# Order of the seven-product pairs, of the weight products and of the weight sums in a one-core decoder layer in float32

## The chip, the cores and the metric

One core of one Trainium2 chip runs the whole program. The metric is the device time of one execution in microseconds; a profiled execution has its own time, and a span from its first to its last instruction. PE is TensorE (its weight loads are listed as PEld), DVE is VectorE, ACT is ScalarE, POOL is GpSimd, SP is SyncE, which here only issues loads.

## The reference

One layer on 256 tokens of width 2048, all in float32:

```
h = rmsnorm(x);  z = h @ W_in            (forgetting attention, mLSTM and two gates)
merged = sigmoid(g_a) * (A @ P_A) + sigmoid(g_m) * (M @ P_M)
x = x + merged @ W_out
u = causal_dwconv3(rmsnorm(x) @ W_up)    (2 x 5632 columns)
x = x + (silu(u_gate) * u_val) @ W_down  (5632 x 2048)
```

The weights are read once; nearly all work is the matrix products.

## The kernel before, in words

**Two halves of each operand.** [...] A weight piece of 128 x 1024 comes from a 1 MB load (`raw`, two pieces each, three buffers, issued by SP); ACT makes the high part `wh` (line 169) and DVE the low part `wl` (line 170, raw minus high). Both have three buffers of 1024 columns. A product of two operands takes three TensorE products: low by high, high by high and high by low.

**Who looks ahead.** `next_sub` hands out the next weight piece and prepares those ahead: two pieces in all in the plain stages, three in the paired ones (`next_sub(3)` in `piece`, line 291). A scheduler then orders each engine's queue by priority and by its own view of when operands and buffers are there; the queues run in that order.

**The stages in order.** First `mog` (mLSTM output gate), then `fq`, `fk`, `fv`, `mq`, `mk`, `mv`, the gates `g0` to `g3`, the projections `p`, `wo0` and `wo1` (W_out), `up` (W_up, 88 blocks of 128 columns), `y0` and `y1` (W_down, 1024 columns each).

- In `mq`, `mk` and `up` (`products_a`, line 258) the weights are the stationary operand: for each of 16 slices of the inner dimension there is one product of 512 columns (high and low activations side by side, against `wh`) and one of 256 columns (high activations against `wl`). They alternate.
- In `g`, `wo` and `y` (`s_block`, line 277) the activations are stationary and the weights move, always 512 columns. The inner dimension goes in pairs of 256 rows. A pattern string says how each pair is multiplied: `p` is plain, eight block products or 24 TensorE products, in two weight pieces; `S` is a scheme with seven block products, 21 TensorE products in four weight pieces. `S` needs differences of weight blocks, which DVE makes in one tile `sums` (lines 154, 161 and 164), and sums of activation blocks.
- For `y` the activation sums are made in `up` by `put_sums`, written to DRAM by POOL, and read back two pairs at a time into tiles `s_ops`, by `load_sums` (line 947), also from POOL.

The pattern of `y` is `ppp` `SSpSp` `SSpSp` `SSpSp` `Sp` `pp`: 22 pairs, ten of them `S`. The patterns of `g1` to `g3` (`pSpSpSpp`) and `wo` (`pSpSpppp`) are not touched.

**The pool `a8`.** Tiles of 8 KB per partition share 15 buffers: among them the four tiles `h2` (normalised activations, read by every block of `up`), the eleven tiles `ghl` (output of `up`, filled one by one), `sums` and the tiles `s_ops`.

**Ends of the `y` stages.** The four sums of seven-product results are combined after the last `S` pair (`late`, two operations for each further weight piece), then the four quarters `q` are added (line 974) and written out by SP.

Of the kernel before, what the change touches and what calls it, by code (L numbers as in the profile page):

```python
# [1 line left out]

# [1 line left out]

# [31 lines left out]
PLAIN = "p" * 8  # L36
G_PAIRS = "pSpSpSpp"
WO_PAIRS = "pSpSpppp"
Y_PAIRS = "ppp" + "SSpSp" * 3 + "Sp" + "pp"
N_S = Y_PAIRS.count("S")  # L40


# [18 lines left out]
def trunk(ctx: ExitStack, tc: tile.TileContext, a):  # L61
# [14 lines left out]
        return psaux.tile([P, 512], F32, tag="aux", name=name)  # L76

    def a8(name, shape, dtype=F32):
        return big.tile([P, *shape], dtype, tag="a8", bufs=15, name=name)

    def scratch(name, shape, tag="w2k", bufs=4):
        return work.tile(shape, F32, tag=tag, bufs=bufs, name=name)
# [51 lines left out]
    def split_sub(j):  # L134
        if j >= len(subs_of) or j in subs:
            return
        i, s, kind = subs_of[j]
        load_chunk(i)
        if j < KD:
            put(hT[j][:, 0, :], hT[j][:, 1, :], xT[j], cst[:, C_G1 + j : C_G1 + j + 1])  # L140
        n = 512 if kind == "b21" else chunks[i][1] // 2
        raw, sums = raws[i], s_tiles.get("sums")


        if kind == "whole":
            src = raw[:, s * n : (s + 1) * n]
        elif kind == "b":
            src = raw[:, 512:1536]
            if s_tiles["of"] != chunks[i][2]:
                s_tiles["of"] = chunks[i][2]  # L150
                s_tiles["sums"] = a8(f"sums{i}", [2048])
            sums = s_tiles["sums"]
            with tc.issue_after(last_of["up"].ins) if "up" in last_of else nullcontext():
                nc.vector.tensor_tensor(  # L154
                    sums[:, :1024].rearrange("p (i c) -> p i c", i=2),
                    raw[:, :512].unsqueeze(1).to_broadcast([P, 2, 512]),
                    src.rearrange("p (i c) -> p i c", i=2), ALU.subtract,
                )
        elif kind == "b21":
            src = raw[:, 1536:]  # L160
            nc.vector.tensor_tensor(sums[:, 1024:1536], raw[:, 1024:1536], sums[:, :512], ALU.subtract)
        elif kind == "t13":
            src = sums[:, :1024]
            nc.vector.tensor_tensor(sums[:, 1536:], raw[:, 1536:], sums[:, 1024:1536], ALU.subtract)
        else:
            src = sums[:, 1024:]
        wh = wpool.tile([P, 1024], F32R, tag="wh", bufs=3, name=f"wh{j}")
        wl = wpool.tile([P, 1024], F32R, tag="wl", bufs=3, name=f"wl{j}")
        nc.scalar.activation(wh[:, :n], src, AF.Copy)  # L169
        nc.vector.tensor_tensor(wl[:, :n], src, wh[:, :n].bitcast(F32), ALU.subtract)  # L170
        subs[j] = (wh[:, :n], wl[:, :n])

    state = {"sub": 0}
# [83 lines left out]

    def products_a(z, act, ks, wh, wl, first, last):

        for q, k in enumerate(ks):  # L260
            ws = slice(q * P, (q + 1) * P)
            mm(z, wh[:, ws], act[k].rearrange("p l s -> p (l s)"), first and q == 0, False)
            mm(z[:, :S], wl[:, ws], act[k][:, 0, :], False, last and q == len(ks) - 1)

    def half_a(z, act, s, tasks_per_sub=1):
        wh, wl = next_sub()
# [10 lines left out]
    def s_block(name, pairs, s_ops, pattern, pools, dst, add=True, per_piece=0):  # L277


        q = [[pools[0](f"{name}q{tok}{h}") for h in range(2)] for tok in range(2)]  # L280
        ps, late, left = {}, [], pattern.count("S")
        n_s = left

        def prod(out, x, w, c, first, last):
            wh, wl = w[0][:, c * 512 : (c + 1) * 512], w[1][:, c * 512 : (c + 1) * 512]
            mm(out, x[1], wh, first, False)
            mm(out, x[0], wh, False, False)
            mm(out, x[0], wl, False, last)

        def piece():  # L290
            w = next_sub(3)
            for _ in range(min(2, len(late))):
                late.pop(0)()
            run_tasks(per_piece)
            return w

        def tt(o, x, y):
            late.append(lambda: nc.vector.tensor_tensor(o, x, y, ALU.add))

        for m, kind in enumerate(pattern):  # L300
            def op(i, tok):
                t = slice(tok * P, (tok + 1) * P)
                return pairs[m][:, i, 0, t], pairs[m][:, i, 1, t]

            if kind == "p":
                last = m == len(pattern) - 1
                ws = [piece(), piece()] if last else []

                todo = (
                    [(i, tok, h) for h in range(2) for tok in range(2) for i in range(2)] if last  # L310
                    else [(i, tok, h) for i in range(2) for h in range(2) for tok in range(2)]
                )
                for i, tok, h in todo:
                    if i == len(ws):
                        ws.append(piece())
                    prod(q[tok][h], op(i, tok), ws[i], 1 - h, m == 0 and i == 0, last and i == 1)
                continue
            first, last = left == n_s, left == 1
            left -= 1
            s1, s2, s3, s4 = s_ops[m]  # L320
            w = piece()
            if first:
                ps = {i: pools[1](f"{name}p{i}") for i in (1, 5, 7, 6)}
            prod(ps[1], op(0, 0), w, 0, first, last)
            prod(q[0][1], s4, w, 1, False, False)
            prod(q[0][0], op(1, 0), piece(), 0, False, False)
            w = piece()
            prod(ps[5], s1, w, 0, first, last)
            prod(ps[7], s3, w, 1, first, last)
            w = piece()  # L330
            prod(ps[6], s2, w, 0, first, last)
            prod(q[1][0], op(1, 1), w, 1, False, False)
            if not last:
                continue
            c11, c12, c21, c22 = (dst(tok, h) for tok in range(2) for h in range(2))
            u2 = scratch("u2", [P, 512])
            if add:
                u3 = scratch("u3", [P, 512])
                late.append(lambda: nc.scalar.activation(u2, ps[1], AF.Copy))
                tt(c11, c11, ps[1])  # L340
                tt(u2, u2, ps[6])
                tt(u3, u2, ps[7])
                tt(u2, u2, ps[5])
                tt(c21, c21, u3)
                tt(u3, u3, ps[5])
                tt(c12, c12, u2)
                tt(c22, c22, u3)
            else:
                late.append(lambda: nc.scalar.activation(c11, ps[1], AF.Copy))
                tt(u2, c11, ps[6])  # L350
                tt(c21, u2, ps[7])
                tt(c12, u2, ps[5])
                tt(c22, c21, ps[5])
        for f in late:
            f()
        return q
# [564 lines left out]
    for j in range(NF):  # L921
# [12 lines left out]
        if Y_PAIRS[m] == "S":  # L934
# [3 lines left out]
                s_dram[:, n_s * 6 * P : (n_s + 1) * 6 * P], se.rearrange("p l c -> p (l c)")  # L938
            )
            n_s += 1  # L940
        last_of["up"] = put_pair(g_pairs[m], gv)


    s_pos = [m for m, kind in enumerate(Y_PAIRS) if kind == "S"]
# [13 lines left out]
        at = [ring[r][:, q * P : (q + 1) * P] for q in range(6 * i, 6 * i + 6)]  # L958
        return [(g[:, 0, 0, P:], g[:, 0, 1, P:])] + [(at[c], at[3 + c]) for c in range(3)]

    for _ in range(2):
        load_sums()
    for b in range(2):
        pools = (acc_tile, aux_tile) if b == 0 else (aux_tile, acc_tile)
        xr = big.tile([P, 2, 1024], F32, tag="mv", name=f"xr{b}")
# [86 lines left out]
```

## Time and profile before

| | us |
|---|---|
| median of 3 runs | 1402.15 |
| lowest and highest run | 1394.18, 1404.11 |
| the profiled execution, its time | 1393.67 |
| the profiled execution, its span | 1391.9 |
| PE busy | 1375.6 |
| DVE busy | 1070.9 |
| ACT busy | 767.2 |

The granted TensorE clock is 1.000 over the span. A matmul's end is modelled in this profile: one of 512 columns is shown as 390 ns or so, though the next one starts sooner. What a stage costs is therefore read here from start to start, and a wait from a start that comes later than the rest, not from the busy shares.

### The profile page before, as it was taken

What the parts mean: (1) busy time and instruction counts of PE and PEld (TensorE: products, weight loads), DVE (VectorE), ACT (ScalarE), POOL (GpSimd) and SP (SyncE); (2) the same over time, 40 slices, a digit from 0 to 9 for tenths busy, and PEclk for the clock granted to TensorE, in tenths of its full rate; (3) what the DMA queues carried; (4) which work ended last, traced back from release to release, by engine and by line L of the source; (5) the groups of instructions that cost most, each with busy time, mean ns of one, the idle gap of its engine ahead of it and who ended that gap; (6) DMA issues with size and microseconds to landing.
All of it is one profiled execution on the core that took longest, in us unless ns stands there. A gap on an engine that the chain in (4) does not pass through costs nothing.

```text
span 1391.9 us, 18433 instructions
## 1 busy us (share of the span) xinstructions
PE 1375.6 (99%) x6940; PEld 1157.2 (83%) x6940; DVE 1070.9 (77%) x1524; ACT 767.2 (55%) x1096; POOL 40.4 (3%) x73
## 2 busy tenths in 40 slices
PE   9999999999999999999999999999999999999998
PEld 8878888887888888888888888888888887778776
DVE  5655766556888867777878888888878888887987
ACT  6645554444665544555655555555655655553553
POOL 2101000000000000000000000000000000000000
PEclk9999999999999999999999999999999999999999
DMA  8645454443554565555555655655555657668553
GB/s 312 229 165 184 179 209 155 152 151 134 196 215 182 214 241 194 190 220 203 191 186 194 218 193 190 222 186 196 201 212 194 230 196 266 226 251 291 205 209 119
DMA packets 44073, 281.76 MB, mean 202 GB/s; under 512 B 5008, under 2 KB 5024, under 8 KB 13264
## 3 DMA queue, kind: packets, MB, share of 16 engines
q1 hardware_dynamic: 39168, 260.20, 52.4%
q0 software_dynamic: 4672, 20.38, 4.2%
q8 instruction: 54, 0.88, 0.2%
q14 instruction: 35, 0.29, 0.1%
q10 hardware_dynamic: 144, 0.02, 0.0%
HBM read 272.45 MB, written 8.13 MB: 202 GB/s over the span
## 4 chain that ended last, share of the span: by engine, by line
PE 96%; DVE 1%; issue 1%; ACT 1%; DMA 1%; POOL 0%; DVEq 0%; ACTq 0%; POOLq 0%
PE up L230 35%; PE p L230 6%; PE y1q L230 6%; PE y0q L230 5%; PE mog L230 3%; PE fq L230 3%; PE mv L230 3%; PE fk L230 3%; PE fv L230 3%; PE wo0q L230 3%; PE wo1q L230 3%; PE g1q L230 2%; PE g3q L230 2%; PE g2q L230 2%; PE g0q L230 2%; PE y1p L230 2%
## 5 line engine op out<-in xcount | busy, mean ns | idle before, releaser
L169 ACT ACTIVATE wh<-raw 128x1024 fp32r<-128x1024 f32 (+2 forms) x496 | 502.7, 1017 | 473.9 <-PE up L230 117.9
L170 DVE TENSOR_TENSOR wl<-raw,wh 128x1024 fp32r<-128x1024 f32 (+2 forms) x496 | 575.1, 1169 | 205.3 <-ACT wh L169 203.5
L230 PE MATMUL up<-h,wh 128*128 128x512 f32 x1408 | 488.6, 394 | 0.0
L230 PE MATMUL up<-h,wl 128*128 128x256 f32 x1408 | 390.0, 277 | 0.0
L230 PEld LDWEIGHTS up<-h,wh 128*128 128x128 f32 x1408 | 263.9, 188 | 61.4 <-DVE h L199 0.2
L230 PEld LDWEIGHTS up<-h,wl 128*128 128x128 f32 x1408 | 264.4, 188 | 0.1
L170 DVE TENSOR_TENSOR wl<-sums,wh 128x1024 fp32r<-128x1024 f32 x66 | 80.6, 1222 | 43.9 <-ACT wh L169 43.5
L169 ACT ACTIVATE wh<-sums 128x1024 fp32r<-128x1024 f32 x66 | 69.9, 1060 | 78.6 <-PE y0q L230 16.6
L909 DVE SCALAR_TENSOR_TENSOR t<-u,cst,t 128x256 f32<-128x256 f32 x176 | 84.7, 481 | 3.8 <-ACT t L907 0.7
L230 PE MATMUL p<-wh,am 128*128 128x512 f32 x256 | 79.6, 392 | 0.0
L230 PE MATMUL y1q<-wh,ghl 128*128 128x512 f32 x232 | 71.7, 390 | 0.0
L230 PE MATMUL y0q<-wh,ghl 128*128 128x512 f32 x232 | 71.7, 390 | 0.0
L230 PEld LDWEIGHTS p<-wh,am 128*128 128x128 f32 x256 | 47.6, 188 | 9.7
L907 ACT ACTIVATE t<-u,cst 128x256 f32<-128x256 f32 x88 | 52.0, 591 | 2.4 <-DVE u L904 1.9
L230 PEld LDWEIGHTS y1q<-wh,ghl 128*128 128x128 f32 x232 | 43.6, 188 | 9.2
L230 PEld LDWEIGHTS y0q<-wh,ghl 128*128 128x128 f32 x232 | 43.5, 188 | 9.1
L230 PE MATMUL p<-wl,am 128*128 128x512 f32 x128 | 49.9, 390 | 0.0
L230 PE MATMUL y1q<-wl,ghl 128*128 128x512 f32 x116 | 44.8, 391 | 0.0
L230 PE MATMUL y0q<-wl,ghl 128*128 128x512 f32 x116 | 44.8, 390 | 0.0
L154 DVE TENSOR_TENSOR sums<-raw 128x1024 f32<-128x1024 f32 x33 | 40.4, 1223 | 4.7 <-DMA raw<-in_w_dn 3.0
L230 PE MATMUL mog<-wh,hT 128*128 128x348 f32 (+1 forms) x192 | 42.4, 331 | 1.3 <-ACT wh L169 1.3
L230 PE MATMUL g0q<-wh,hN 128*128 128x512 f32 x128 | 41.3, 401 | 0.0
(370 smaller groups left out, 2064.0 us busy)
## 6 DMA issues: line engine op xcount, KB each, us to landing
raw<-in_w_up SPq DMA_DIRECT2D x88, 1024.0 KB, 4.9
raw<-in_w_dn SPq DMA_DIRECT2D x44, 1024.0 KB, 4.9
raw<-in_w_g SPq DMA_DIRECT2D x32, 1024.0 KB, 4.9
raw<-in_w_fox SPq DMA_DIRECT2D x24, 1024.0 KB, 4.9
raw<-in_w_p SPq DMA_DIRECT2D x16, 1024.0 KB, 4.8
raw<-in_w_out SPq DMA_DIRECT2D x16, 1024.0 KB, 4.8
raw<-in_w_mqk SPq DMA_DIRECT2D x8, 1024.0 KB, 4.8
raw<-in_w_mv SPq DMA_DIRECT2D x8, 1024.0 KB, 4.8
```

The source lines that it names most:

```text
L154: nc.vector.tensor_tensor(sums[:, :1024].rearrange("p (i c) -> p i c", i=2), raw[:, :512].unsqueeze(1).to_broadcast([P, 2, 512]), src.rear ...
L169: nc.scalar.activation(wh[:, :n], src, AF.Copy)
L170: nc.vector.tensor_tensor(wl[:, :n], src, wh[:, :n].bitcast(F32), ALU.subtract)
L230: nc.tensor.matmul(out, lhsT, rhs, start=start, stop=stop)
L907: nc.scalar.activation(t, u[:, 2:], AF.Identity, scale=w[2], bias=w[3])
L909: nc.vector.scalar_tensor_tensor(out=t, in0=u[:, i : i + S], scalar=w[i], in1=t, op0=ALU.mult, op1=ALU.add)
```

## The change

Five edits:

1. `Y_PAIRS` becomes `p`, ten times `Sp`, `p`: still 22 pairs and ten `S`, now at every second place.
2. `wh` and `wl` have four buffers in place of three, and `s_block` prepares four pieces ahead.
3. The pool `a8` has 14 buffers in place of 15, and one `s_ops` tile is loaded ahead in place of two.
4. The first operation of a seven-product pair's sums is queued behind the last low part issued so far (`issue_after`), in every paired stage; before, it was held only behind the last activation pair of `up`.
5. `products_a` takes two slices at a time: two products of 512 columns, then their two of 256.

```diff
-Y_PAIRS = "ppp" + "SSpSp" * 3 + "Sp" + "pp"
+Y_PAIRS = "p" + "Sp" * 10 + "p"
...
-        return big.tile([P, *shape], dtype, tag="a8", bufs=15, name=name)
+        return big.tile([P, *shape], dtype, tag="a8", bufs=14, name=name)
...
-            with tc.issue_after(last_of["up"].ins) if "up" in last_of else nullcontext():
+
+            with tc.issue_after(last_of["wl"].ins):
...
-        wh = wpool.tile([P, 1024], F32R, tag="wh", bufs=3, name=f"wh{j}")
-        wl = wpool.tile([P, 1024], F32R, tag="wl", bufs=3, name=f"wl{j}")
+        wh = wpool.tile([P, 1024], F32R, tag="wh", bufs=4, name=f"wh{j}")
+        wl = wpool.tile([P, 1024], F32R, tag="wl", bufs=4, name=f"wl{j}")
         nc.scalar.activation(wh[:, :n], src, AF.Copy)
-        nc.vector.tensor_tensor(wl[:, :n], src, wh[:, :n].bitcast(F32), ALU.subtract)
+        last_of["wl"] = nc.vector.tensor_tensor(
+            wl[:, :n], src, wh[:, :n].bitcast(F32), ALU.subtract
+        )
...
-        for q, k in enumerate(ks):
-            ws = slice(q * P, (q + 1) * P)
-            mm(z, wh[:, ws], act[k].rearrange("p l s -> p (l s)"), first and q == 0, False)
-            mm(z[:, :S], wl[:, ws], act[k][:, 0, :], False, last and q == len(ks) - 1)
+
+        for q in range(0, len(ks), 2):
+            two = [(slice(i * P, (i + 1) * P), act[ks[i]]) for i in (q, q + 1)]
+            for i, (ws, x) in enumerate(two):
+                mm(z, wh[:, ws], x.rearrange("p l s -> p (l s)"), first and q + i == 0, False)
+            for i, (ws, x) in enumerate(two):
+                mm(z[:, :S], wl[:, ws], x[:, 0, :], False, last and q + i == len(ks) - 1)
...
-            w = next_sub(3)
+            w = next_sub(4)
...
-        last_of["up"] = put_pair(g_pairs[m], gv)
+        put_pair(g_pairs[m], gv)
...
-    for _ in range(2):
-        load_sums()
+    load_sums()
```

Three places show how the queues move. The first is PE inside a block of `up`. Before:

```order
L230 MATMUL up_5923<-h_4789,wh_5893 128x512
L230 MATMUL up_5923<-h_4789,wl_5894 128x256
L230 MATMUL up_5923<-h_4789,wh_5893 128x512
L230 MATMUL up_5923<-h_4789,wl_5894 128x256
L230 MATMUL up_5923<-h_4789,wh_5893 128x512
```

and now (x2: two rows that read alike):

```order
L233 MATMUL up_6199<-h_4789,wh_6168 128x512 x2
L233 MATMUL up_6199<-h_4789,wl_6169 128x256 x2
L233 MATMUL up_6199<-h_4789,wh_6168 128x512 x2
L233 MATMUL up_6199<-h_4789,wl_6169 128x256 x2
L233 MATMUL up_6199<-h_4790,wh_6202 128x512 x2
```

The products are the same and as many; only their order in a group of four differs, and each still has a weight load of its own.

The second is DVE in `y0`. The number behind `raw` is the load, that behind `wl` the piece; four pieces belong to an `S` pair and two to a `p` pair. Before, at the second of two adjacent `S` pairs (`raw208`):

```order
L170 TENSOR_TENSOR wl442_10452<-sums207_10411,wh442_10451 128x1024
L154 TENSOR_TENSOR sums207_10411<-raw208_10409 128x1024
L170 TENSOR_TENSOR wl443_10466<-sums207_10411,wh443_10465 128x1024
L170 TENSOR_TENSOR wl444_10474<-raw208_10409,wh444_10473 128x1024
L161 TENSOR_TENSOR sums207_10411<-raw208_10409,sums207_10411 128x512
L170 TENSOR_TENSOR wl445_10485<-raw208_10409,wh445_10484 128x512
L164 TENSOR_TENSOR sums207_10411<-raw208_10409,sums207_10411 128x512
L170 TENSOR_TENSOR wl446_10498<-sums207_10411,wh446_10497 128x1024
L170 TENSOR_TENSOR wl447_10508<-sums207_10411,wh447_10507 128x1024
```

and now, from a `p` pair (`raw206`) through an `S` pair (`raw207`) to the next `p` pair (`raw208`):

```order
L171 TENSOR_TENSOR wl440_10400<-raw206_10335,wh440_10399 128x1024
L171 TENSOR_TENSOR wl441_10407<-raw206_10335,wh441_10406 128x1024
L155 TENSOR_TENSOR sums205_10341<-raw207_10383 128x1024
L171 TENSOR_TENSOR wl442_10418<-raw207_10383,wh442_10417 128x1024
L162 TENSOR_TENSOR sums205_10341<-raw207_10383,sums205_10341 128x512
L171 TENSOR_TENSOR wl443_10431<-raw207_10383,wh443_10430 128x512
L165 TENSOR_TENSOR sums205_10341<-raw207_10383,sums205_10341 128x512
L171 TENSOR_TENSOR wl444_10448<-sums205_10341,wh444_10447 128x1024
L171 TENSOR_TENSOR wl445_10466<-sums205_10341,wh445_10465 128x1024
L171 TENSOR_TENSOR wl446_10476<-raw208_10427,wh446_10475 128x1024
L171 TENSOR_TENSOR wl447_10483<-raw208_10427,wh447_10482 128x1024
```

The eight operations of an `S` pair are the same; what stands between two such groups is now always the two low parts of a `p` pair.

The third is ACT at the end of `up` (blocks up84 to up87 are its last; `wh434` is the first piece of `y0`). Before:

```order
L169 ACTIVATE wh430_10190<-raw202_10115 128x1024
L195 ACTIVATE ghl10_5500<-gv_10005 128x2x256
L360 ACTIVATE sum_10157<-up84_10114 128x256
L169 ACTIVATE wh431_10223<-raw202_10115 128x1024
L907 ACTIVATE t_10161<-u0_5502,cst_75 128x256
L169 ACTIVATE wh432_10243<-raw203_10168 128x1024
```

and now:

```order
L170 ACTIVATE wh435_10337<-raw204_10221 128x1024
L366 ACTIVATE sum_10263<-up86_10220 128x256
L198 ACTIVATE ghl10_5504<-gv_10005 128x2x256
L170 ACTIVATE wh436_10343<-raw205_10274 128x1024
L913 ACTIVATE t_10267<-u2_5508,cst_75 128x256
L170 ACTIVATE wh437_10348<-raw205_10274 128x512
L933 ACTIVATE sg_10271<-t_10267 128x256
L366 ACTIVATE sum_10316<-up87_10273 128x256
L170 ACTIVATE wh438_10365<-sums205_10341 128x1024
```

With 14 buffers the eleventh `ghl` tile takes the place of the first `h2` tile that block up87 has finished with, so its first half is written two blocks later than before; `sums` and the first `s_ops` tile take the next `h2` tiles in the same way. Behind it on ACT's queue stand the pieces of the first `S` pair of `y0` (`wh436` to `wh439`).

More of the change, by code (lines that the diff above doesn't have):

```diff
@@ L1 @@
-from contextlib import ExitStack, nullcontext
+from contextlib import ExitStack
 import numpy as np
```

## Prediction

> **What bounds the kernel now.** I read the page first: engines, then the chain that ended last.
>
> ```profile
> span 1391.9 us, 18433 instructions
> PE 1375.6 (99%) x6940; PEld 1157.2 (83%) x6940; DVE 1070.9 (77%) x1524; ACT 767.2 (55%) x1096; POOL 40.4 (3%) x73
> PE 96%; DVE 1%; issue 1%; ACT 1%; DMA 1%; POOL 0%; DVEq 0%; ACTq 0%; POOLq 0%
> ```
>
> TensorE holds the chain for 96% of the span. No edit removes a product, so only two things can be won: stretches in which PE stands still, and time lost between products. To see the stretches I need the step of an undisturbed stream. The timeline of PE, in the projections:
>
> ```profile
> 499.67 0.39 PE L230 MATMUL p<-wh,am 128*128 128x512 f32 x1
> ...
> 500.58 0.39 PE L230 MATMUL p<-wl,am 128*128 128x512 f32 x1
> ```
>
> Four products lie between these starts (the rows left out hold the second, third and fourth): 0.91/4 = 0.227 us a step for 512 columns. Then the view by tile, which gives first and last starts of a stage's products:
>
> ```profile
> L230 PE MATMUL g1q<-wh,hN x92: 387/389/400, 356.1 to 397.4; 128*128 128x512 f32 x92
> L230 PE MATMUL g2q<-wh,hN x92: 387/389/397, 397.9 to 439.5; 128*128 128x512 f32 x92
> L230 PE MATMUL y0q<-wh,ghl x232: 387/389/399, 1150.7 to 1269.3; 128*128 128x512 f32 x116
> L230 PE MATMUL y1q<-wh,ghl x232: 387/389/398, 1269.8 to 1386.7; 128*128 128x512 f32 x116
> ```
>
> A `y` stage has 12 plain pairs of 24 products and 10 `S` pairs of 21: 498 products, 113.0 us at 0.227. `y0` takes 1269.8 - 1150.7 = 119.1 us, so **6.1 us** are lost. `y1`, from its first start to 1386.7, where its last but one product starts, takes 116.9 us for 496 steps (112.6): **4.3 us** lost. Together 10.4. The stage `g1`, with three `S` pairs that each stand alone, has 183 products (41.5 us) and takes 397.9 - 356.1 = 41.8 us: 0.3 us lost, a tenth of a microsecond for each `S`.
>
> Where `y0` loses is in the timelines. PE, ACT and DVE at the second of two adjacent `S` pairs:
>
> ```profile
> 1174.48 0.63 PE L230 MATMUL y0p<-wh,s_ops 128*128 128x512 f32 x2
> 1175.92 0.51 PE L230 MATMUL y0p<-wh,s_ops 128*128 128x512 f32 x1 [0.81 <-ACT wh L169]
> ```
>
> ```profile
> 1174.81 1.06 ACT L169 ACTIVATE wh<-sums 128x1024 fp32r<-128x1024 f32 x1 [1.90 <-DVE sums L164]
> ```
>
> ```profile
> 1169.39 1.23 DVE L154 TENSOR_TENSOR sums<-raw 128x1024 f32<-128x1024 f32 x1
> 1170.54 1.22 DVE L170 TENSOR_TENSOR wl<-sums,wh 128x1024 fp32r<-128x1024 f32 x1
> 1171.67 1.22 DVE L170 TENSOR_TENSOR wl<-raw,wh 128x1024 fp32r<-128x1024 f32 x1
> 1172.81 0.68 DVE L161 TENSOR_TENSOR sums<-raw,sums 128x512 f32<-128x512 f32 x1
> 1173.41 0.68 DVE L170 TENSOR_TENSOR wl<-raw,wh 128x512 fp32r<-128x512 f32 x1
> 1174.01 0.68 DVE L164 TENSOR_TENSOR sums<-raw,sums 128x512 f32<-128x512 f32 x1
> 1174.61 2.51 DVE L170 TENSOR_TENSOR wl<-sums,wh 128x1024 fp32r<-128x1024 f32 x2
> 1177.04 1.22 DVE L170 TENSOR_TENSOR wl<-raw,wh 128x1024 fp32r<-128x1024 f32 x1
> ```
>
> Three starts of PE fit from 1174.48 to 1175.92, 1.44 us for two steps of 0.227: about 1 us stands still. It waits for a high part on ACT, which waits for the last sum on DVE, and DVE is the one that is late: from start to start its `S` group takes 1.15 + 1.14 + 0.60 + 0.60 + 0.60 + 2.43 = 6.5 us, against 21 x 0.227 = 4.8 us of PE. Two in a row put DVE 3.4 us behind. A `p` pair gives DVE 2 x 1.14 = 2.3 us of work in 24 x 0.227 = 5.4 us, which makes that good. The waits of both `y` stages, grouped:
>
> ```profile
> ACT wh L169 <- DVE sums L164: 11.4, 6, 1.9
> PEld y0p L230 <- DVE wl L170: 3.7, 10, 1.9
> PEld y0p L230 <- ACT wh L169: 3.7, 3, 1.2
> PEld y1p L230 <- ACT wh L169: 3.7, 3, 1.2
> PEld y1p L230 <- DVE wl L170: 2.1, 10, 0.3
> ```
>
> Six such waits for the six adjacent pairs, three per stage. The rows that count ten are a small wait at every `S`; the 1.9 us one in `y0` comes, in the chain of waits, behind a weight load that DVE released late:
>
> ```profile
> 1232.65 7.81 DMA raw<-in_w_dn
> ```
>
> **The change part by part.** The sum is against the profiled execution, 1393.67 us: the span of 1391.9 and 1.8 around it. That execution lies at the bottom of the runs shown (1394.18 to 1404.11, median 1402.15); I carry the difference over to the median.
>
> *One `S` at every second place.* Per `Sp` DVE works 6.5 + 2.3 = 8.8 us and PE 4.8 + 5.4 = 10.2 us, so DVE gains 1.4 us with each, and no `S` starts behind another. The six stops go, and the load of 1232.65, whose buffer was freed late by the same backlog, comes in time. What should be left is what `g1` shows, 0.1 us for each of 20 `S`: 2 us; with four buffers it may fall to nothing, because a high part then no longer waits for the piece just before. Of 10.4 us lost, 8.4 come back.
>
> *The start of `y0`.* The first `S` is now at the second place. The covers are used up here: at the end of `up`, DVE and ACT still finish two blocks, and the `sums` and `s_ops` tiles come only from `h2` tiles that block up87 leaves. ACT's queue stands for the first `ghl` half until the first `h2` tile is free, a quarter into that block, some 1 us; behind it are `wh436` to `wh439`, needed from 1150.7 + 5.4 = 1156.1 on, so this is hidden. The `s_ops` tile is needed at the second product group, 1156.1 + 0.7 = 1156.8. Before, the first went out here:
>
> ```profile
> 1147.02 0.57 POOL L952 DMA_DIRECT2D s_ops<-s_dram  x1 [43.80 <-PE up L230]
> ```
>
> ```profile
> DMA to landing us min/median/max: 4.4/4.7/10.6
> ```
>
> Now it waits for the third `h2` tile (the first goes to `ghl`, the second to `sums`), three quarters into up87, which takes 5.5 us to 1150.7: 1149.3, and 0.6 to issue. With the median it lands at 1154.6 and costs nothing; with the maximum at 1160.5 it costs 3.7. A weight load and the second `s_ops` run beside it, which puts it between: I take **0.7 us lost**, and 0 to 3.7 as ends.
>
> *From `y0` to `y1`.* Behind the last `S` come two `p` pairs and the first of `y1`, then again an `S`. The additions of line 974 wait for the last products, and the first sums of `y1` are queued behind them; but they are needed two pieces into a stage, 5.4 us later. I cost it at nothing; if that cover were gone, two additions and two sums, 4 x 0.6 = 2.4 us.
>
> *One `s_ops` ahead, 14 buffers elsewhere.* A tile serves two `S`, 20.4 us, and takes 4.7 to land: hidden. Before `up` the queues shift by single rows; 0, and 1 either way.
>
> *Sums behind low parts, four ahead, in `g` and `wo`.* `g1` loses 0.3 us as above, and `g2` 0.5 (397.9 to 439.5 is 41.6 us, for 181 steps that make 41.1), so little is to be had: 0.3 us gained, 0 to 1.
>
> *Products in groups of four.* There are 88 x 16 = 1408 pairs in `up` and 128 in `mq` and `mk`: 768 groups. The alternation, and a place where the scheduler happens to have put two and two:
>
> ```profile
> 799.89 0.39 PE L230 MATMUL up<-h,wh 128*128 128x512 f32 x1
> 800.12 0.27 PE L230 MATMUL up<-h,wl 128*128 128x256 f32 x1
> ...
> 801.62 0.40 PE L230 MATMUL up<-h,wh 128*128 128x512 f32 x1
> ```
>
> ```profile
> 665.50 0.40 PE L230 MATMUL up<-h,wh 128*128 128x512 f32 x1
> 665.86 0.62 PE L230 MATMUL up<-h,wh 128*128 128x512 f32 x2
> 666.32 0.40 PE L230 MATMUL up<-h,wl 128*128 128x256 f32 x2
> 666.55 0.40 PE L230 MATMUL up<-h,wh 128*128 128x512 f32 x1
> ```
>
> Five pairs from 799.89 to 801.62 are 0.346 us each, 0.692 for two. A 512 step is 0.23 there against 0.227 in `p`; half of 0.227 and the whole make 0.3405, so 5.5 ns a pair are lost to something. If a neighbour of the other length costs them, groups of four save half: 5.5 ns x 768 = 4.2 us. If every product has the same fixed cost, they save nothing. The group of four in the trace takes 666.55 - 665.86 = 0.69 us: no gain against two settled pairs, 0.03 against its neighbour pair (665.86 - 665.50 = 0.36). So the ends are 0 and 4.2, nearer 0: **1.3 us gained**.
>
> [...]
>
> Sum: -8.4 + 0.7 - 0.3 - 1.3 = **-9.3 us**: 1384.4 beside the profiled 1393.67, and 1402.15 - 9.3 = **1392.9** beside the median.
>
> **The rivals.**
>
> *The order of the products is worth nothing.* Every product has its fixed cost; the one group of four speaks for it, the longer 0.23 against it. Time 1392.9 + 1.3 = 1394.2.
>
> *The order is worth more.* All that `up`, `mq` and `mk` lose between unlike products goes: 5.5 ns x 1536 = 8.4 us in place of 1.3, so 1385.8. The group of four speaks against it.
>
> *`y` keeps half its losses.* The tile `sums` is still single, and DVE is busy for most of the stage:
>
> ```profile
> 1150.70:1269.80 119.10, 115.24 (x501) 91.82 (x500) 101.80 (x112) 63.56 (x69) 3.19 (x6) 1.00 0.68 246
> ```
>
> 101.8 of 119.1 us. If the late `s_ops` tile costs its 3.7 and each `S` still loses 0.2 us (4 of the 10.4), the sum is -6.4 + 3.7 - 0.3 - 1.3 = -4.3: 1397.9. Against it stands `g1`, with the same `Sp` and less buffering.
>
> *Slower: two short products in a row uncover a weight load.* The costliest groups show how long a load lasts:
>
> ```profile
> L230 PEld LDWEIGHTS up<-h,wl 128*128 128x128 f32 x1408 | 264.4, 188 | 0.1
> ```
>
> 188 ns, and a 256 step is 0.115. Were the second load of two not hidden, each group would pay 188 - 115 = 73 ns, 768 x 73 = 56 us: 1449 us. It decides from (9.3 - 1.3)/768 = 10 ns a group on, where the gain is gone. The two short products from 666.32 to 666.55, 0.115 each, speak against it; and in the alternation too each short product covers one whole load.
>
> *Nothing changes.* The stops of `y` move elsewhere, as into the load queue: 1402.
>
> **How the numbers follow.** Chances: the forecast 0.42, the order worth nothing 0.24, the order worth more 0.10, half the losses 0.15, slower 0.04, nothing 0.05. The likeliest time is 1392.9. The runs of before spread over 10 us, so the range takes the cases from 1385.8 to 1397.9 and some 3 to 4 us of that spread on each side: 1382 to 1401. A change of 1%, 14 us, is about what a measurement of this kernel tells from none. Faster than that (under 1388.1) are the third case and what the spread makes of the first two, 0.20; slower by 1% only the fifth, 0.05; within 1%, 0.75.
>
> **What would show it.** In the profile after: `y0` and `y1` at 114 to 115 us each, no wait of ACT for DVE's third sum that PE feels, and no PE start more than 0.4 us late at an `S`. `up` from first to last start at 487 to 489 us if order is worth little, 480 if it is worth all, over 500 if loads are uncovered. The first `s_ops` landing before 1157. Wrong would be: `y` still over 117 us, or a new stop of several microseconds between `up` and the first `S`.

## The result, and the profile after

The changed kernel takes **1380.98 us** (median of 6 runs, 1380.65 to 1381.26); the kernel before, beside it, 1404.01 (6 runs, 1394.18 to 1405.35). The ratio is 0.985, 95% interval 0.982 to 0.987: faster by 1.5%. The forecast was 1392.9, and its range ended at 1382, one microsecond above the result.

The page of the changed kernel (span, engines, chain that ended last):

```profile
span 1379.4 us, 18385 instructions
PE 1369.1 (99%) x6940; PEld 1161.6 (84%) x6940; DVE 1069.6 (78%) x1524; ACT 766.7 (56%) x1096; POOL 40.9 (3%) x73
PE 96%; issue 1%; DMA 1%; DVE 1%; POOL 1%; ACT 0%; SPq 0%; DVEq 0%; ACTq 0%; POOLq 0%
```

The shares are as before; what has changed is when products start. The view by tile, with the first and last starts of a stage's products:

```profile
L233 PE MATMUL g1q<-wh,hN x92: 389/389/389, 354.5 to 395.5; 128*128 128x512 f32 x92
L233 PE MATMUL g2q<-wh,hN x92: 389/389/389, 396.0 to 437.0; 128*128 128x512 f32 x92
L233 PE MATMUL up<-h,wh x1408: 388/396/582, 657.9 to 1148.5; 128*128 128x512 f32 x176
L233 PE MATMUL up<-h,wl x1408: 274/277/287, 658.5 to 1148.9; 128*128 128x256 f32 x176
L233 PE MATMUL y0q<-wh,ghl x232: 389/389/395, 1149.0 to 1261.4; 128*128 128x512 f32 x116
L233 PE MATMUL y1q<-wh,ghl x232: 389/389/389, 1261.9 to 1374.3; 128*128 128x512 f32 x116
L233 PE MATMUL y1q<-wl,ghl x116: 388/389/389, 1262.3 to 1374.5; 128*128 128x512 f32 x116
```

`y0` takes 1261.9 - 1149.0 = 112.9 us (119.1 before); both `y` stages, from the first start of `y0` to the last of `y1`, 1374.5 - 1149.0 = 225.5 (before 1386.9 - 1150.7 = 236.2, its last start being that of the row below). That is 995 steps of 0.227: nothing is lost. `g1` takes 41.5 (41.8 before), also without loss. But `up` takes 1148.9 - 657.9 = 491.0, where before it took 488.7:

```profile
L230 PE MATMUL up<-h,wl x1408: 274/280/284, 662.2 to 1150.6; 128*128 128x256 f32 x176
L230 PE MATMUL y1q<-wl,ghl x116: 387/389/445, 1270.2 to 1386.9; 128*128 128x512 f32 x116
```

From the profiled execution of before to that of after, the span falls by 12.5 us. The medians differ by 23.0. Ten microseconds are thus not to be seen between these two profiles, and the experiments had to find them too.

DVE's timeline in `y0`, at one `S` pair:

```profile
1175.95 1.23 DVE L171 TENSOR_TENSOR wl<-sums,wh 128x1024 fp32r<-128x1024 f32 x1 [1.26 <-ACT wh L170]
1177.32 2.36 DVE L171 TENSOR_TENSOR wl<-raw,wh 128x1024 fp32r<-128x1024 f32 x2
1179.59 1.22 DVE L155 TENSOR_TENSOR sums<-raw 128x1024 f32<-128x1024 f32 x1
1180.73 1.22 DVE L171 TENSOR_TENSOR wl<-raw,wh 128x1024 fp32r<-128x1024 f32 x1
...
1183.67 1.22 DVE L171 TENSOR_TENSOR wl<-sums,wh 128x1024 fp32r<-128x1024 f32 x1
1186.15 1.23 DVE L171 TENSOR_TENSOR wl<-sums,wh 128x1024 fp32r<-128x1024 f32 x1 [1.26 <-ACT wh L170]
```

DVE now finishes the `S` pair, does the two low parts of the `p` pair and then begins the next sums, with 1.3 us to spare in each round (its wait for ACT). An `S` pair gives it seven operations, three sums and four low parts, not eight as the text ahead of the prediction has it; the 6.5 us of the prediction are those of the seven. The load of the first `s_ops` tile was feared to be late. POOL issues it at 1146.66, it lands 7.1 us later, at 1153.7, and PE first uses it at 1155.12:

```profile
1146.66 0.56 POOL L958 DMA_DIRECT2D s_ops<-s_dram  x1 [26.45 <-PE up L233]
```

```profile
1154.89 0.39 PE L233 MATMUL y0p<-wl,ghl 128*128 128x512 f32 x1
1155.12 0.62 PE L233 MATMUL y0q<-wh,s_ops 128*128 128x512 f32 x2
```

That product follows the one before it at the usual step of 0.23 us.

### The profile page after: what moved, and what is told of

Read it like the earlier page. It is cut to its first block, busy times and chain, and to the rows that moved or that the text cites. A ratio compares the mean times of both kernels' runs of the same rounds, so it can differ in the third digit from the quotient of the medians.

```text
span 1379.4 us, 18385 instructions
## 1 busy us (share of the span) xinstructions
PE 1369.1 (99%) x6940; PEld 1161.6 (84%) x6940; DVE 1069.6 (78%) x1524; ACT 766.7 (56%) x1096; POOL 40.9 (3%) x73
## 4 chain that ended last, share of the span: by engine, by line
PE 96%; issue 1%; DMA 1%; DVE 1%; POOL 1%; ACT 0%; SPq 0%; DVEq 0%; ACTq 0%; POOLq 0%
PE up L233 36%; PE p L233 6%; PE y1q L233 6%; PE y0q L233 6%; PE fq L233 3%; PE mv L233 3%; PE fk L233 3%; PE fv L233 3%; PE wo0q L233 3%; PE wo1q L233 3%; PE g0q L233 3%; PE g3q L233 2%; PE g1q L233 2%; PE g2q L233 2%; PE y1p L233 2%; PE y0p L233 2%
## 5 line engine op out<-in xcount | busy, mean ns | idle before, releaser
L233 PE MATMUL up<-h,wh 128*128 128x512 f32 x1408 | 442.4, 396 | 0.0
L233 PE MATMUL up<-h,wl 128*128 128x256 f32 x1408 | 276.5, 278 | 0.0
L233 PEld LDWEIGHTS up<-h,wh 128*128 128x128 f32 x1408 | 214.5, 189 | 0.6 <-DVE h L202 0.5
L233 PE MATMUL mv<-wh,hT 128*128 128x512 f32 x128 | 40.2, 395 | 0.0
```

Of the source, the lines that this page charges most:

```text
L233: nc.tensor.matmul(out, lhsT, rhs, start=start, stop=stop)
```

## The experiments

Each compares with the kernel before on the same chip, and each kernel has one profiled execution: `y` and `up` are its, while the medians are of several runs. "y" below is the time from the first start of `y0` to the last start of `y1`, "up" that from its first to its last start.

### The kernel before, again

No edit.

> The kernel before, unchanged, to see where its runs at 1404 us lose the 10 us that those at 1394 us do not. Theory A: the 10 us arise in y, where DVE stays behind through the adjacent S pairs and one weight load (the one of 1232.65 us) is already issued late; a 1404 profile then shows y0 and y1 together some 10 us over 119.1 + 117.1, and the stages ahead of y as before. Theory B: they arise in the stages ahead of y (three weight buffers); then first y0 start is some 10 us later than 1150.7 and y is as before. Theory C: they are spread in proportion over the span (as a clock would make them): 0.7% on every stage. A profile at 1394 again would leave this open.

1402.64 us (10 runs: four at 1392.35 to 1395.35, six at 1402.03 to 1404.18). The profile fell on the lower level and left the question open; its y is 237.9, 1.7 more than in the first profile, by one more stop of 1.6 us, and `up` is 488.7 in both. The two levels are plain, though: of 82 runs of this kernel in all, 25 took 1392.1 to 1395.8, 57 took 1401.3 to 1405.8, and none lies between.

### The new pattern alone

```diff
-Y_PAIRS = "ppp" + "SSpSp" * 3 + "Sp" + "pp"
+Y_PAIRS = "p" + "Sp" * 10 + "p"
```

> Only the pattern of y is changed; three buffers, the sums still held only behind the last activation pair, alternating products. Theory A (the spacing of the S pairs is what y gains by): y0 and y1 at 113 to 115 us each from first to last start, that is 8 to 10 us less than 119.1 + 117.1 together, less up to 4 us at the first S of y0; span 1382 to 1386, and no run near 1404. Rival (the fourth buffer is what y gains by): y keeps more than half of its 10.4 us lost, span over 1387.

**1414.63 us, slower**: ratio 1.007 (1.005 to 1.009). y takes 246.4 us, 10.2 more than before. My theory was wrong. PE and DVE at one of its stops:

```profile
1193.85 1.07 PE L230 MATMUL y0q<-wh,ghl 128*128 128x512 f32 x4
1196.76 0.50 PE L230 MATMUL y0p<-wl,s_ops 128*128 128x512 f32 x1 [1.85 <-DVE wl L170]
```

```profile
1191.04 1.23 DVE L170 TENSOR_TENSOR wl<-sums,wh 128x1024 fp32r<-128x1024 f32 x1 [1.52 <-ACT wh L169]
1194.35 1.23 DVE L154 TENSOR_TENSOR sums<-raw 128x1024 f32<-128x1024 f32 x1 [2.08 <-DMA raw<-in_w_dn]
1195.49 1.22 DVE L170 TENSOR_TENSOR wl<-sums,wh 128x1024 fp32r<-128x1024 f32 x1
```

Four products from 1193.85 end their steps at 1194.76; the next starts 2.0 us later. It needs the fourth low part of this `S` pair. On DVE's queue the first sum of the *next* `S` pair stands ahead of that low part, and that sum waits for a load until 1194.35. Seven stops of 1.6 to 2.8 us, 14 us in all, stand in the two stages, and at six of them PE waits for that low part. Behind one of them in `y0` the products also run for a while at a granted clock of 0.53, and shown as up to 628 ns; so are some in `y1` (last section). DVE had enough time, and stood still in the wrong place.

The same profile showed what nothing had prepared me for: `up` takes 497.9 us in it, with code that is the same as before's. The row with its last start (its first is at 663.4):

```profile
L230 PE MATMUL up<-h,wl x1408: 274/281/284, 663.7 to 1161.3; 128*128 128x256 f32 x176
```

### The products alone

```diff
-        for q, k in enumerate(ks):
...
+        for q in range(0, len(ks), 2):
+            two = [(slice(i * P, (i + 1) * P), act[ks[i]]) for i in (q, q + 1)]
...
```

> Only the products of up, mq and mk go in groups of four. Theory A (a product costs its columns plus a fixed part, whatever its neighbour, and a group of four even a little more): up from first to last start 491 us against 488.8, all else as before, and the 1404 level still there: median 1396 or 1406 by the level. Rival (the order saves what I forecast, and something else in the changed kernel makes up longer): up at 487 us or less.

1396.27 us, all four runs between 1395.05 and 1396.82. `up` takes 490.9, 2.2 more than in the profile of before, as expected. What I had not expected: the level of 1404 is gone, though four runs are few. So, if the upper level is the `up` of 497.9 seen with the pattern alone, in a run on before's lower level the groups of four cost 2 us, and in one on its upper level they win 7.

### Buffers and held sums, without the pattern and the products

```diff
-Y_PAIRS = "p" + "Sp" * 10 + "p"
+Y_PAIRS = "ppp" + "SSpSp" * 3 + "Sp" + "pp"
...
-        for q in range(0, len(ks), 2):
+        for q, k in enumerate(ks):
...
```

(against the changed kernel)

> Four buffers with four pieces ahead, the pool of 14, one s_ops tile ahead and the sums behind low parts, with the old pattern of y and alternating products. Theory A (spacing): the adjacent pairs still put DVE 3.4 us behind; one more buffer takes up part of it, y loses 3 to 8 us of its 10.4, and the stages g1 to g3 and wo and mog gain 3.6 us together: span 1381 to 1387. Rival (the fourth buffer alone does it, since the deficit of two S pairs fits into one more piece ahead): y loses under 2 us, span 1378 to 1381, 2 us below the changed kernel for the alternating products. On the level of 1404: if it is gone here and not with the pattern alone, it belongs to the three buffers.

1382.11 us, three runs at 1382.0 to 1382.1 and one at 1391.14; span 1380.2. y takes 228.5, that is 2.6 us lost, in three small waits at each adjacent pair and none over 0.3 us. That lies between the two theories, and the span is the rival's: with the old pattern the fourth buffer takes up nearly all of the deficit of two adjacent `S` pairs. The stages ahead of `up` begin it at 657.9, as in the changed kernel. The run at 1391 shows that buffers, pool and hold do not end the two levels.

### The changed kernel with alternating products

```diff
-        for q in range(0, len(ks), 2):
+        for q, k in enumerate(ks):
...
```

> The changed kernel with the products of up, mq and mk alternating again. Theory D, from the runs so far: the alternating stream settles in each execution on one of two steps, 0.346 us a pair (up 488.6 us, as in the profiles of before) or 0.353 (up 497.8, as in that of the pattern alone), and groups of four always take 0.697 for two pairs; the 10 us between the levels of before are 1536 x 6.6 ns. Then this kernel has two levels, 1378.8 us (1381.0 less 2.2) and 1388 to 1389, and up in the profile is 488 to 489 or 497 to 498, nothing between; at the upper level the changed kernel is some 7 us faster than this one. Rival (the levels belong to the three buffers or the old pattern): all runs at 1378 to 1380.

Four runs at 1378.9 to 1379.1, two at 1388.2 and 1388.3; the profile is of one of the latter. Both levels are where theory D put them, and `up` takes 497.8:

```profile
L233 PE MATMUL up<-h,wh x1408: 392/398/585, 658.1 to 1155.6; 128*128 128x512 f32 x176
L233 PE MATMUL up<-h,wl x1408: 274/281/284, 658.4 to 1155.9; 128*128 128x256 f32 x176
```

PE's timeline at its start shows the stream change its step, where two products of another kind come between:

```profile
667.30 0.39 PE L233 MATMUL up<-h,wh 128*128 128x512 f32 x1
...
669.03 0.40 PE L233 MATMUL up<-h,wh 128*128 128x512 f32 x1
669.26 0.28 PE L233 MATMUL up<-h,wl 128*128 128x256 f32 x1
669.38 0.59 PE L233 MATMUL ps_rb<-dg,ones 128*128 128x256 f32 x2
...
670.16 0.40 PE L233 MATMUL up<-h,wh 128*128 128x512 f32 x1
...
671.94 0.40 PE L233 MATMUL up<-h,wh 128*128 128x512 f32 x1
```

Five pairs from 667.30 to 669.03 are 0.346 us each; five from 670.16 to 671.94 are 0.356 (0.353 over a longer stretch), and so it stays to the end of `up`. In before's profile the same two products, at 673 us, change the step the other way, from 0.353 to 0.347.

### Pattern and held sums, three buffers

```diff
-        return big.tile([P, *shape], dtype, tag="a8", bufs=14, name=name)
+        return big.tile([P, *shape], dtype, tag="a8", bufs=15, name=name)
...
-        wh = wpool.tile([P, 1024], F32R, tag="wh", bufs=4, name=f"wh{j}")
-        wl = wpool.tile([P, 1024], F32R, tag="wl", bufs=4, name=f"wl{j}")
+        wh = wpool.tile([P, 1024], F32R, tag="wh", bufs=3, name=f"wh{j}")
+        wl = wpool.tile([P, 1024], F32R, tag="wl", bufs=3, name=f"wl{j}")
...
-            w = next_sub(4)
+            w = next_sub(3)
...
-    load_sums()
+    for _ in range(2):
+        load_sums()
```

(against the changed kernel; products alternating as well)

> Before with the new pattern and the sums held behind the last low part, but three buffers, three pieces ahead, two s_ops tiles ahead and alternating products. Theory E (the pattern alone lost 10 us in y because DVE took the first sum of the next S pair, and its wait for the load, ahead of the low parts of the present one; the hold mends that): no stop of 1.6 us or more in y, y0 and y1 at 113 to 115 us each. Rival (three buffers cannot carry the pattern): stops of over 1 us at most S pairs, y0 and y1 at 117 us or more. Ahead of y as before; the level of up decides the rest, span 1384 or 1393.

1393.29 us, all five runs within 1 us of each other; the profiled one has the long step (`up` 497.9). `y0` and `y1`:

```profile
L233 PE MATMUL y0q<-wh,ghl x232: 387/389/403, 1159.6 to 1273.1; 128*128 128x512 f32 x116
L233 PE MATMUL y1q<-wh,ghl x232: 387/389/398, 1273.5 to 1386.8; 128*128 128x512 f32 x116
L233 PE MATMUL y1q<-wl,ghl x116: 387/389/398, 1274.0 to 1387.0; 128*128 128x512 f32 x116
```

113.9 us and 113.5: y is 227.4, no stop is over 0.2 us, and three buffers carry the pattern. Against the pattern alone the hold is worth 19 us of y, the stretches at the lower clock included.

### The changed kernel with groups of sixteen

```diff
-        for q in range(0, len(ks), 2):
-            two = [(slice(i * P, (i + 1) * P), act[ks[i]]) for i in (q, q + 1)]
...
+        xs = [(slice(i * P, (i + 1) * P), act[k]) for i, k in enumerate(ks)]
+        for i, (ws, x) in enumerate(xs):
+            mm(z, wh[:, ws], x.rearrange("p l s -> p (l s)"), first and i == 0, False)
+        for i, (ws, x) in enumerate(xs):
+            mm(z[:, :S], wl[:, ws], x[:, 0, :], False, last and i == len(xs) - 1)
```

> The changed kernel with the products of a piece in groups of sixteen: eight of 512 columns, then their eight of 256. Theory F (what is lost beside 0.227 and 0.1135 us is lost where the length changes, and a quarter as often now): 8 x 0.341 + 4 x 6 ns at the most, up at 481 to 485 us, median 1371 to 1375. Rival (every product has its own fixed loss, whatever its neighbour): up stays at 490 to 492, median 1380 to 1382. Second rival (the weight loads of 188 ns are not hidden behind eight products of 0.115 us): each of 704 blocks of products in the half blocks loses up to 7 x 73 ns, up over 500, some 90 us longer at worst.

1382.31 us (1382.22 to 1382.52), `up` 492.2:

```profile
L233 PE MATMUL up<-h,wh x1408: 387/393/577, 657.7 to 1148.8; 128*128 128x512 f32 x176
L233 PE MATMUL up<-h,wl x1408: 277/283/283, 661.0 to 1149.9; 128*128 128x256 f32 x176
```

Theory F falls: fewer changes of length win nothing. The rival with a fixed loss for every product is the near one, though `up` is 1.2 longer than with groups of four. Weight loads are not uncovered either: eight short products in a row take 0.95 us, 0.12 each, with a load of 192 ns (median) for each of them.

### The changed kernel without the hold

```diff
-            with tc.issue_after(last_of["wl"].ins):
+            with tc.issue_after(last_of["up"].ins) if "up" in last_of else nullcontext():
...
```

> The changed kernel without the hold of the sums behind the last low part (they are held only behind the last activation pair of up, as before); pattern, four buffers and groups of four stay. Theory E (the hold is what makes the pattern safe): stops of 1 to 2.7 us at several S pairs of y, as with the pattern alone; y0 and y1 at 116 to 126 us each; up as in the changed kernel, 491; median 1387 to 1400. Rival (the fourth buffer alone is enough): y0 and y1 at 113 to 115, median 1381 to 1383.

1397.04 us (1393.79 to 1401.17): y is 241.3, with stops of 2.0, 1.8 and 3.1 us (the last followed by a granted clock of 0.53), eight waits of 0.3 to 0.5 us, and the same picture as with the pattern alone. DVE ahead of the stop that ends at 1293:

```profile
1290.56 1.23 DVE L155 TENSOR_TENSOR sums<-raw 128x1024 f32<-128x1024 f32 x1 [4.52 <-DMA raw<-in_w_dn]
1291.70 1.22 DVE L171 TENSOR_TENSOR wl<-sums,wh 128x1024 fp32r<-128x1024 f32 x1
```

It waits 4.5 us for a load at a first sum, the needed low part behind it. So with this pattern the hold is needed even with four buffers: 15.8 us of y.

### One group of four per piece

```diff
-        for q in range(0, len(ks), 2):
...
+        for i, lo in [(0, 0), (1, 0), (0, 1), (1, 1)]:
+            one(i, lo)
+        for i in range(2, len(ks)):
+            one(i, 0)
+            one(i, 1)
```

(`one` issues the product of 512 columns, or that of 256)

> The changed kernel with one group of four at the start of each piece of up, mq and mk and six alternating pairs behind it. In the traces so far the alternating stream keeps its step for 480 us and changes it only where two other products come between (at 673 us in before, at 669 us with the alternating products). Theory G (the step is the phase that the last interruption left): the group of four interrupts 176 times in up and always alike, so all runs fall on one level: with 0.3468 us a pair behind it, a piece takes 0.697 + 6 x 0.3468 = 2.778 and up 488.9 us, median 1379.1; with 0.3533, 2.817 and 495.8, median 1386. Rival (the step is given to the whole execution by something outside the stream): two levels, 1379 and 1386, as with pure alternation.

1382.76 us, all six runs within 0.13 us. PE's timeline over two pieces:

```profile
902.34 0.40 PE L233 MATMUL up<-h,wh 128*128 128x512 f32 x1
...
904.42 0.62 PE L233 MATMUL up<-h,wh 128*128 128x512 f32 x2
904.88 0.40 PE L233 MATMUL up<-h,wl 128*128 128x256 f32 x2
905.11 0.40 PE L233 MATMUL up<-h,wh 128*128 128x512 f32 x1
...
907.23 0.63 PE L233 MATMUL up<-h,wh 128*128 128x512 f32 x2
```

Six pairs take 2.08 us in the first piece and 2.12 in the next, and in turn so through nearly all of `up`. Each group of four changes the step of the pairs behind it, so the execution has half of each, and `up` takes 492.6, 2.80 a piece, the mean of the two. Of theory G the one level holds; its two times, 1379.1 and 1386, do not, for that the step would change in turn I had not foreseen.

### The held sums alone

```diff
-            with tc.issue_after(last_of["up"].ins) if "up" in last_of else nullcontext():
+            with tc.issue_after(last_of["wl"].ins):
...
```

(against the kernel before)

> Before with the hold of the sums behind the last low part as its only edit: old pattern, three buffers, alternating products. Theory E (the hold keeps DVE from taking a sum that waits for its load ahead of low parts that PE needs; the adjacent pairs lose by DVE's pace, which the hold does not change): the stop of 1.6 us in y0 goes, five or six stops of 1 us stay, y0 and y1 at 117 to 118 each, span 1390 at the lower step of up. Rival (the hold is all that y gains by): y0 and y1 at 113 to 115.

1401.29 us, ratio 1.001 (0.998 to 1.004): nothing, as expected. y is 235.2; the stop of 1.6 us is gone, and six of 1.0 us are left. Eight of its ten runs are at 1400.4 to 1401.6 and two at 1391.6 and 1391.9; the profile is of one at 1401.33, and its `up` takes 497.9:

```profile
L232 PE MATMUL up<-h,wl x1408: 274/281/284, 661.6 to 1159.2; 128*128 128x256 f32 x176
```

This is the nearest that a profile comes to the upper level of before itself: the products are its own, y is no longer than before's, and the time that is more lies in `up`.

### The buffers alone

```diff
-        wh = wpool.tile([P, 1024], F32R, tag="wh", bufs=3, name=f"wh{j}")
-        wl = wpool.tile([P, 1024], F32R, tag="wl", bufs=3, name=f"wl{j}")
+        wh = wpool.tile([P, 1024], F32R, tag="wh", bufs=4, name=f"wh{j}")
+        wl = wpool.tile([P, 1024], F32R, tag="wl", bufs=4, name=f"wl{j}")
...
-            w = next_sub(3)
+            w = next_sub(4)
```

(against the kernel before, and edit 3 with it)

> Before with the four buffers, four pieces ahead, the pool of 14 and one s_ops tile ahead as its only edits: old pattern, no hold ahead of y, alternating products. Theory E (buffers without the hold let DVE take a waiting sum even earlier): y keeps stops of 1 to 3 us, y0 and y1 at 117 or more each, span 1388 or more at the lower step of up; the gain in mog, g1 to g3 and wo of 3.6 us is there without the hold. Rival (the fourth buffer absorbs the deficit by itself): y0 and y1 at 114 each as with buffers and hold together, span 1380.

**1382.43 us** (1381.70 to 1384.92), ratio 0.990 (0.987 to 0.994). y:

```profile
L230 PE MATMUL y0q<-wh,ghl x232: 387/389/402, 1146.7 to 1259.8; 128*128 128x512 f32 x116
L230 PE MATMUL y1q<-wh,ghl x232: 389/389/398, 1260.3 to 1375.0; 128*128 128x512 f32 x116
L230 PE MATMUL y1q<-wl,ghl x116: 388/389/395, 1260.7 to 1375.2; 128*128 128x512 f32 x116
```

228.5 us, with one stop of 2.1 at 1297.54, again behind a sum that waits for its load. My expectation for y was wrong, and the rival right: with the fourth buffer and four pieces ahead (not tried apart) the six stops are gone. That y is 228.5 with the hold too is chance: there it is many small waits, here mostly the one stop. The stages ahead of `up` gain what they gain in the changed kernel, as expected. The profiled run has the short step of `up`, and by their times so have the other four; of the kernel with the same buffers and the hold, one run of four is 9 us longer.

### Pieces that begin in turn with 512 and with 256 columns

```diff
-        for q in range(0, len(ks), 2):
...
+        flip = ks[0] > 0
+        for q, k in enumerate(ks):
...
+            for lo in (flip, not flip):
...
```

> The changed kernel with alternating products, in which every second piece of a block begins with its product of 256 columns: 512, 256, ... in the first piece of 16 products, 256, 512, ... in the second, so that two products of one length meet at each border of pieces. With one group of four per piece the trace showed the step of the six pairs behind it change at every group, 2.080 us, then 2.120, in turn through all of up. Theory G (an interruption shifts the phase, and the phase sets the step): here too the step is set anew at each border; all runs fall on one level, and up is 488 to 489 if a border always leaves the short step, 497 to 498 if the long one, 492 to 494 if it changes in turn; median 1379, 1388 or 1383. Rival (the step is given to the execution from outside): two levels, 1379 and 1388.

1383.12 us, all six runs within 0.4 us, `up` 493.0: one level, of the kind with both steps in turn (two pieces at 2.78 us, two at 2.81 to 2.82). None of the orders tried holds the short step for good. The changed kernel's groups of four give the best time that comes in every run, 1381; pure alternation gives 1379 in four runs of six and 1388 in two.

## Why the prediction was right or wrong

The sum of -9.3 was made against the profiled execution, where the change is -12.4 (1393.67 to 1381.26). By its steps:

**The stops of `y`: -8.4 predicted, -10.7 measured, and for a reason that was half wrong.** I gave the whole of it to the spacing. The edits tried by themselves and together give this, y in microseconds of one execution each ("four buffers" is edits 2 and 3; before's second profile has 237.9, so differences of 1 or 2 say little):

| | three buffers | four buffers |
|---|---|---|
| old pattern | 236.2 (before) | 228.5 |
| old pattern, sums held | 235.2 | 228.5 |
| new pattern | 246.4 | 241.3 |
| new pattern, sums held | 227.4 | 225.5 (changed kernel) |

The new pattern without the hold loses 10 to 13 us; with it, it gains 3 to 8. The step that failed is the one from "no `S` starts behind another" to "The six stops go": it counted DVE's work per pair (8.8 against 10.2 us, which holds) and not what stands ahead of what on DVE's queue. The spacing alone made seven stops, 246.4 us, with a sum that waits for its load ahead of the low part that PE needs. I costed the hold at 0.3 us and only in `g` and `wo`; it is what the new pattern rests on. Nor is the spacing needed: the old pattern with four buffers is down to 228.5. Edits 2 and 3 by themselves take the span from 1391.9 to 1380.1, 11.8 of the 12.5 us between the profiles of before and after; pattern and hold then add 3.0 in y, and the groups of four take 2.2 of it back in `up`. The residual, 0.1 us for each `S`, was well read for three buffers (227.4 is 1.5 over the 225.9 of 995 steps); with four it is nothing, as the prediction said it might be.

**The start of `y0`: +0.7 predicted, 0 measured.** The first `s_ops` tile goes out 2.6 us earlier than the 1149.3 that I worked out, 1.7 of them because `y0` itself begins that much earlier (1149.0 against 1150.7). It takes 7.1 us to land, more than the median of 4.7 that I used, and is in time all the same. The second goes out here:

```profile
1149.46 0.53 POOL L958 DMA_DIRECT2D s_ops<-s_dram  x1 [2.23 <-PE up L233]
```

**From `y0` to `y1`: 0 predicted, 0 measured**: from 1261.7, its last start, to 1261.9 is one step.

**`g` and `wo`: -0.3 predicted (0 to -1).** Measured: `g1` to `g3` 1.2 (125.7 to 124.5), `wo` 1.1, and 1.3 by the end of `mog`, which I had not looked at: -3.6. The fourth buffer served not only stages that prepare four pieces: in `mog`, which prepares two, ACT's waits for PE to free a weight buffer fall from 6.4 us to 2.3:

```profile
ACT wh L169 <- PE mog L230: 6.4, 7, 1.2
```

```profile
ACT wh L170 <- PE mog L233: 2.3, 3, 1.1
```

The first row is before, the second after. The kernel with edits 2 and 3 alone, where `up` begins at 657.8 (657.9 in the changed kernel, 661.9 before), shows that all of this is theirs.

**The products: -1.3 predicted, +2.2 measured in `up` and -0.3 in `mq` and `mk`**, on the step of the profile of before. The term took 5.5 ns a pair for a loss between unlike products, which grouping would halve. It is not such a loss: against the short step groups of four cost 2.2 us in `up`, groups of sixteen 3.4. Order is not worth nothing either: one and the same order has two steps, and none tried has the same sum as another (`up` at 488.7 or 497.9 alternating, 491.0 in fours, 492.2 in sixteens, 492.6 and 493.0 mixed).

The sum came near the -12.4 in part by luck: `y`, its start and the stages ahead of `up` came out 6.3 us better than I put them, the products 3.2 us worse.

**Beside the median: the carrying over failed.** I took the spread of 10 us between before's runs for chance scatter and put the difference on the median. It is two values of one step, 0.347 and 0.353 us a pair, kept through nearly all of the 1408 pairs of `up`: 1408 x 6.6 ns = 9.3 us, against 497.8 - 488.7 = 9.1 measured. Both profiles of before have the short one. That its 57 runs of 82 on the upper level have the long one is concluded, not seen: from the distance of the levels, and from the profiles of the kernels with the pattern alone, with pattern and hold, and with the hold alone, which all show 497.9. In the changed kernel's groups of four all six runs lie within 0.6 us, so -12.4 became -23.0. The size depends on which levels before's runs drew: on one chip 11 of 18 were on the lower one, and the median was 1395.3. The rival "the order is worth more" (0.10) came nearest to the median, by luck: what groups of four win is 497.9 - 491.0 = 6.9 us against the long step, and not the loss between unlike products on which it rested.

**The tests.** The two stages came out at 112.9 and 112.6, below the 114 to 115 named, and no two starts in `y` lie more than 0.233 us apart, so that none is late at an `S`; the first `s_ops` landed at 1153.7, before the 1157 named; `up` at 491.0, above the 487 to 489 that stood for an order of little worth. No weight load was uncovered (a group of four takes 491.0/704 = 0.697 us; 73 ns more, as the prediction put it, would be 0.77), no stop stands between `up` and the first `S`.

What stays open: why a pair has two steps, and what decides in an execution which one it gets. Shown is only that the step changes at interruptions and lasts until the next; a phase of the stream, as theory G has it, is a name for that and was not measured. The times of the two kernels with the pattern and without the hold scatter (1403.1 to 1419.4 and 1393.8 to 1401.2), so the sizes of their losses in y are not firm.

## What to carry to other kernels

An in-order queue is costed by what stands in front of the needed instruction and what that waits for, and only then by its share of busy time: an edit that gives an engine more time can lose by it when it moves a wait on a load ahead of work that is due (here y at 246.4 us in place of 236.2, by the pattern alone). Where runs of a kernel fall on two levels (here 1392.1 to 1395.8 and 1401.3 to 1405.8), find out which one the profile shows before a difference is carried from it to the median. And a buffer that an edit adds in a shared pool is to be counted in every stage that uses the pool: here edits 2 and 3 alone let `up` begin at 657.8 in place of 661.9.

## What the runs showed of the hardware

**The alternating stream of `up` ran with two steps, and the one gave way to the other where something came between.** Products of 512 and 256 columns in turn, each with its own weight load, ran at 0.347 or 0.353 us a pair. Where two products of another kind came between, the step went from 0.353 to 0.347 in the profile of before (at 673 us), and from 0.346 to 0.353 in the changed kernel with alternating products (at 669 us); in the kernel with one group of four per piece it changed at each group (six pairs in 2.08 us, then in 2.12). In a stream of groups of four alone two pairs take 0.697 in all three profiles that have it (`up` at 490.9 to 491.0 for 704 groups).

**Behind one stop of 3.1 us and one of 2.0 the granted clock was 0.53.** In the kernel without the hold PE stands still from 1289.9 to 1293.0; the windows ahead of the stop, behind it and after the clock's return (time, PE, weight loads, DVE, ACT, POOL, then the granted clock):

```profile
1283.00:1289.60 6.60, 6.60 (x31) 5.47 (x30) 3.04 (x5) 4.13 (x4) 0.00 (x0) 1.00 1.01 395
1293.00:1299.30 6.30, 6.30 (x16) 4.96 (x17) 5.13 (x6) 0.63 (x1) 1.06 (x2) 0.53 0.66 221
1299.30:1305.00 5.70, 5.70 (x27) 4.71 (x26) 3.83 (x4) 3.49 (x4) 0.00 (x0) 1.00 0.99 396
```

At 0.53 there are 16 products in 6.3 us, where 6.6 us held 31 ahead of it. Their 15 steps would take 3.4 us at 0.227, so by this estimate the stop of 3.1 us costs some 2.9 more. With the pattern alone the stop of 2.0 us that ends at 1196.76 was followed by the same:

```profile
1197.00:1200.40 3.40, 3.40 (x9) 2.61 (x9) 3.40 (x4) 0.85 (x1) 0.00 (x0) 0.53 0.19 27
```

The seven steps from 1196.76 to 1199.58 take 2.8 us in place of 1.6, so that stop of 2.0 us cost at least 1.2 more. In `y1` of that profile too a product is shown as up to 628 ns, as in `y0` (389 in the median of both). Not every such stop was followed by it: in the kernel with the buffers alone, whose stop of 2.1 us ends at 1297.54, no product of `y1q` is shown as over 398 ns. What decides is not shown.
